# Sums, differences and residuals around the block products: from GpSimd to VectorE

## The chip, the cores and the metric

One core of one Trainium2 chip runs the whole program. A core has TensorE (PE, matrix products), VectorE (DVE), ScalarE (ACT), GpSimd (POOL), SyncE (SP, which here issues the DMAs), an on-chip memory SBUF, and the banks PSUM into which TensorE writes. Each engine takes its instructions in one fixed order and waits at each until its inputs are there. The metric is device time in microseconds (us) of one execution, less is better.

## The reference

One layer of a hybrid decoder for 2048 tokens of width 1024, in float32:

```python
h = rms_norm(x, norm_mix) * (1 + sc1) + sh1        # shifts, scales, gates from silu(c) @ w_ada
z = h @ w_in                                       # 1024 -> q, k, v of 12 + 4 heads, and two gates
ya = dilated_mixture(qa, ka, va) @ w_up_a          # windowed attention, three dilations, merged
yb = forgetting_attention(qb, kb, vb, fz, b_forget) @ w_up_b
x = x + g1 * ((sigmoid(gza) * ya + sigmoid(gzb) * yb) @ w_out)
h = rms_norm(x, norm_ffn) * (1 + sc2) + sh2
gate, up = split(h @ w_ffn_in)                     # 1024 -> 2 x 2816
x = x + g2 * ((silu(gate) * up) @ w_ffn_out)       # 2816 -> 1024
out = rms_norm(x, norm_final)
```

## The kernel before

Five phases follow each other: 1, the projection by `w_in`; 2, the two attentions and their merge; 3, `w_out` with the residual and the second norm; 4, `w_ffn_in` with silu; 5, `w_ffn_out` with the residual and the last norm.

**Precision.** A float32 operand is split into a high part, rounded by ScalarE (line 108), and a low part, the rest, which VectorE subtracts (line 109, `split`). A product then takes three matmuls (lines 102 to 104, `mm3`).

**Seven products for eight.** Phases 1, 3, 4 and 5 multiply 2x2 blocks with seven block products in place of eight (Strassen's scheme in Winograd's form). The price is sums and differences of blocks before and after the products.
- On the resident side, `a_prep` makes seven operands A11, A12, S1, S2, S3, A22, S4 of (usually) four 128x512 tiles each. Such a *preparation* is 28 splits, and per tile the sum for S1 (line 181), two differences on the way to S2 and S3 (183, 185) and two for S4 (192). There is one at each of: the start of phase 1 (tiles `a_`, written out at lines 353 to 376), its second half, phase 3 (`wo_`), the two halves of phase 4 (`f_`), and the three thirds of phase 5 (`w_`; the first with three tiles for four). The code gives a slot to every resident tile once, so a preparation writes a tile as soon as the products of the stage before have read it.
- On the streamed side, `b_ops` makes for each block four differences `wt` (line 219) and splits seven operands into `wh` and `wl`. Of `wh` and of `wl` there are six slots, so splits run at most six products ahead. One product is 12 matmuls of 512 columns, one block 84.
- Behind the products, ScalarE copies partial sums out of PSUM (`keep`, line 246: `p`, `u`), VectorE adds them to later ones. In phases 3 and 5 `residual` adds the old `x` to the copy (line 1026) and then to the product (1027); in phase 4 `up_` multiplies by the silu (1098).
- `scaled` loads a tile `ws` of an output weight, multiplies it by a gate (line 566) and stores it, eight rows in the gate blocks of phase 1, 22 in phase 4.

**Who does what.** In the kernel before GpSimd makes S1's sum and S3's difference, all `wt`, the `scaled` products, the residual's first sum, the silu's product, and the low part of one tile in each preparation of phase 4. In phase 2 it makes attention biases (815, 820) and parts of the merge (966, 968, 992).

**Order.** The program is traced in the order of the code and then put in order by a scheduler that works with its own estimates of times. The same code with an operation on another engine is thus put in another order, on all engines.

Of the kernel before, what the change touches and what calls it, by code (L numbers as in the profile page):

```python
# [37 lines left out]

PRODUCTS = {1: "A11", 2: "A12", 3: "S4", 4: "A22", 5: "S1", 6: "S2", 7: "S3"}
ORDER = (1, 2, 5, 6, 7, 4, 3)  # L40

GL4 = (("A11", 3),)

SEGS = {"A": ("pc",), "F": ("wh", "wl")}
SCT = {"A": "X", "F": "Z", "E": "XZ", "U": "X"}
# [16 lines left out]
def trunk(ctx, tc, x, c, w_ada, b_ada, norm_mix, w_in, b_forget, w_up_a, w_up_b, w_out,  # L62
# [40 lines left out]
        PE.matmul(o, lh, rl, start=False, stop=False, skip_group_check=True)  # L103
        PE.matmul(o, ll, rh, start=False, stop=last, skip_group_check=True)  # L104

    def split(hi, lo, src, sub=None):

        A.activation(hi, src, AF.Copy)  # L108
        (sub or V).tensor_tensor(lo, src, raw(hi), op=ALU.subtract)  # L109

    def rstd_of(ss, n, nm):

# [54 lines left out]
            t.setdefault(n, []).append(slot("big" if i < 11 else "bigx", nm + n + s, [P, nk, CH], F32R))  # L167
        return t

    def a_prep(t, get, nk=4, gl=()):  # L170


        def sp(n, k, p):
            split(t[n][0][:, k, :], t[n][1][:, k, :], p, G if (n, k) in gl else None)
        for k in range(nk):
            sp("A11", k, get(0, k))
        for k in range(nk):
            sp("A12", k, get(0, k + nk))
        for k in range(nk):
            pb, pb4, pa, s1 = get(1, k), get(1, k + nk), get(0, k), slot("pc", "s1")  # L180
            G.tensor_tensor(s1, pb, pb4, op=ALU.add)
            sp("S1", k, s1)
            V.tensor_tensor(s1, s1, pa, op=ALU.subtract)  # L183
            sp("S2", k, s1)
            G.tensor_tensor(pb, pa, pb, op=ALU.subtract)
            sp("S3", k, pb)
        for k in range(nk):
            sp("A22", k, get(1, k + nk))
        for k in range(nk):
            p = get(0, k + nk)  # L190
            for part in t["S2"]:
                V.tensor_tensor(p, p, raw(part)[:, k, :], op=ALU.subtract)  # L192
            sp("S4", k, p)
# [15 lines left out]
    def b_ops(groups, shape, lockstep=False):  # L209

        f = lambda a: a[:, :shape[0] * shape[1]].rearrange("p (a b) -> p a b", a=shape[0])
        vs = [{1: b11, 2: b21, 3: b22} for b11, b21, b12, b22 in groups]
        made = {5: lambda g, v: (g[2], g[0]), 6: lambda g, v: (g[3], v[5]), 7: lambda g, v: (g[3], g[2]),
                4: lambda g, v: (g[1], v[6])}

        def make(i, g, v):
            if i in made:
                v[i] = f(slot("wt", f"wt{i}"))
                G.tensor_tensor(v[i], *made[i](g, v), op=ALU.subtract)  # L219
        if len(groups) == 1 or not lockstep:  # L220
            for g, v in zip(groups, vs):
                for i in (5, 6, 7, 4):
                    make(i, g, v)
        ops = [{} for _ in groups]
        for i in ORDER:
            for g, v, o in zip(groups, vs, ops):
                if i not in v:
                    make(i, g, v)
                o[i] = f(slot("wh", "wh", dt=F32R)), f(slot("wl", "wl", dt=F32R))
                split(*o[i], v[i])  # L230
        return ops
# [129 lines left out]
    for k in range(4):  # L361
        for kk in (k, k + 4):
            A.activation(pb[kk], x_t(xb, kk), AF.Identity, bias=S1[:, kk:kk + 1], scale=A1[:, kk:kk + 1])
        G.tensor_tensor(s1[k], pb[k], pb[k + 4], op=ALU.add)
        sp("S1", k, s1[k])
    for k in range(4):
        V.tensor_tensor(s1[k], s1[k], pa[k], op=ALU.subtract)
        sp("S2", k, s1[k])
    for k in range(4):
        G.tensor_tensor(pb[k], pa[k], pb[k], op=ALU.subtract)  # L370
        sp("S3", k, pb[k])
    for k in range(4):
        sp("A22", k, pb[k + 4])
# [185 lines left out]
    def scaled(w, dst, k, row, hold_):  # L559

        for n in range(2):
            ns = slice(n * CH, (n + 1) * CH)
            p = slot("pc", "ws")
            with tc.issue_after(hold_):
                SP.dma_start(p, w[k * P:(k + 1) * P, ns])
            G.tensor_tensor(p, p, row[n], op=ALU.mult)  # L566
            SP.dma_start(dst[k * P:(k + 1) * P, ns], p)

    for i, (jL, jR) in enumerate(QK_PAIRS):
# [450 lines left out]
    def residual(xs, o, kept, i, n, out_=None):  # L1020

        xt = xs[i][n]
        if kept is None:
            V.tensor_tensor(xt, o, xt, op=ALU.add)
        else:
            G.tensor_tensor(kept, kept, xt, op=ALU.add)  # L1026
            V.tensor_tensor(xt, o, kept, op=ALU.add)  # L1027
        return xt

# [46 lines left out]
    for hf in range(2):  # L1076
        at4 = a_tiles(f"f{hf}_")
        a, b = 2 * hf, 2 * hf + 1
        a_prep(at4, from_dram(h2sp, a, b), gl=GL4)

        def p4_block(f):
            sil = {}

            def c11(o, kept):
                t = slot("s", "ga")
                V.tensor_tensor(t, o, kept, op=ALU.add)
                A.activation(t, t, AF.Silu)
                sil["a"] = t

            def c21(o):  # L1090
                t = slot("s", "gb")
                A.activation(t, o, AF.Silu)  # L1092
                sil["b"] = t

            def up_(o, kept, ci, which):
                t = slot("t", "ac")
                V.tensor_tensor(t, o, kept, op=ALU.add)  # L1097
                G.tensor_tensor(t, t, sil[which], op=ALU.mult)  # L1098
                SP.dma_start(act_scr[ci][f], t)
            return (kcols(w_ffn_in, f * P, P), kcols(w_ffn_in, DFF + f * P, P),  # L1100
                    c11, lambda o, t: up_(o, t, a, "a"), c21, lambda o, t: up_(o, t, b, "b"))
# [90 lines left out]
```

## Time and profile before

| | |
|---|---|
| median of three runs | 2989.59 us (2987.12 to 2991.21) |
| profiled execution, its own time | 2990.01 us |
| its span (first to last instruction) | 2988.30 us |
| TensorE busy | 2789.4 us, 93% |
| VectorE busy | 1906.6 us, 64% |
| ScalarE busy | 1371.7 us, 46% |
| GpSimd busy | 1359.1 us, 45% |

Busy time of an engine is the union of its instructions' spans. TensorE is without work for 199 us of the span; the mean hides that these lie in a few stretches.

### The profile page before, as it was taken

What the parts mean: (1) busy time and instruction counts of PE and PEld (TensorE: products, weight loads), DVE (VectorE), ACT (ScalarE), POOL (GpSimd) and SP (SyncE); (2) the same over time, 40 slices, a digit from 0 to 9 for tenths busy, and PEclk for the clock granted to TensorE, in tenths of its full rate; (3) what the DMA queues carried; (4) which work ended last, traced back from release to release, by engine and by line L of the source; (5) the groups of instructions that cost most, each with busy time, mean ns of one, the idle gap of its engine ahead of it and who ended that gap; (6) DMA issues with size and microseconds to landing.
All of it is one profiled execution on the core that took longest, in us unless ns stands there. A gap on an engine that the chain in (4) does not pass through costs nothing.

```text
span 2988.3 us, 41178 instructions
## 1 busy us (share of the span) xinstructions
PE 2789.4 (93%) x13666; PEld 2311.8 (77%) x13666; DVE 1906.6 (64%) x3509; ACT 1371.7 (46%) x2722; POOL 1359.1 (45%) x1077
## 2 busy tenths in 40 slices
PE   4899999999999999788798999999999999989898
PEld 3689887978887889676586788887788887868676
DVE  7865478476537887787667744337633338694987
ACT  3554335344447777652355533334333334433443
POOL 2323234323532222654645565545644436564642
PEclk7999999999999999999899999999999999989999
DMA  7487466467856757479566544444422236775642
GB/s 247 121 219 224 131 208 195 145 169 190 266 183 241 238 182 241 115 223 327 192 206 205 182 152 138 141 141 138 138 85 85 85 102 196 216 229 162 194 155 96
DMA packets 488414, 530.54 MB, mean 178 GB/s; under 512 B 58596, under 2 KB 339580, under 8 KB 481276
## 3 DMA queue, kind: packets, MB, share of 16 engines
q1 hardware_dynamic: 488200, 527.91, 56.4%
q8 instruction: 107, 1.75, 0.2%
q14 instruction: 107, 0.88, 0.1%
HBM read 356.51 MB, written 171.29 MB: 177 GB/s over the span
## 4 chain that ended last, share of the span: by engine, by line
PE 41%; DVE 6%; issue 2%; DMA 2%; POOL 1%; ACT 1%; SPq 0%; DVEq 0%; POOLq 0%; ACTq 0%
PE psX L102 8%; PE psX L103 8%; PE psX L104 7%; PE psZ L102 4%; PE psZ L104 4%; PE psZ L103 4%; PE psY L103 2%; PE psY L102 2%; PE psY L104 2%; DVE wl L109 1%; DVE pc L192 1%; POOL wt L219 1%; DMA x<-x 1%; DVE s L183 0%; DVE x L1027 0%
## 5 line engine op out<-in xcount | busy, mean ns | idle before, releaser
L109 DVE TENSOR_TENSOR wl<-wt,wh 128x512 fp32r<-128x512 f32 (+1 forms) x464 | 396.2, 859 | 414.8 <-ACT wh L108 388.8
L108 ACT ACTIVATE wh<-wt 128x512 fp32r<-128x512 f32 (+1 forms) x464 | 288.1, 622 | 622.1 <-PE psX L103 273.7
L219 POOL TENSOR_TENSOR wt<-wr,wt 128x512 f32<-128x512 f32 (+1 forms) x216 | 319.5, 1480 | 402.8 <-DVE wl L109 339.5
L219 POOL TENSOR_TENSOR wt<-wr 128x512 f32<-128x512 f32 (+1 forms) x216 | 310.7, 1438 | 286.8 <-DVE wl L109 222.3
L109 DVE TENSOR_TENSOR wl<-wr,wh 128x512 fp32r<-128x512 f32 (+1 forms) x324 | 274.7, 851 | 209.8 <-ACT wh L108 199.0
L108 ACT ACTIVATE wh<-wr 128x512 fp32r<-128x512 f32 (+1 forms) x324 | 201.1, 621 | 414.1 <-PE psX L103 233.5
L815 POOL TENSOR_SCALAR bi<-nf,F_col 128x512 f32<-128x512 f32 (+3 forms) x160 | 106.8, 671 | 232.4 <-DVE mx L829 204.9
L1026 POOL TENSOR_TENSOR u<-u,x 128x512 f32<-128x512 f32 x64 | 92.9, 1455 | 93.5 <-ACT u L246 83.8
L246 ACT ACTIVATE u<-psX 128x512 f32<-128x512 f32 x216 | 125.5, 581 | 5.8 <-PE psX L104 5.8
L1098 POOL TENSOR_TENSOR ac<-ac,gb 128x512 f32<-128x512 f32 x44 | 61.2, 1390 | 139.3 <-ACT gb L1092 139.3
L1097 DVE TENSOR_TENSOR ac<-psZ,u 128x512 f32<-128x512 f32 x88 | 60.4, 686 | 89.2 <-PE psZ L104 89.0
L839 ACT ACTIVATE L<-L,nmf 128x512 f32<-128x512 f32 (+3 forms) x160 | 103.3, 648 | 19.2 <-DVE nmf L835 19.2
L1098 POOL TENSOR_TENSOR ac<-ac,ga 128x512 f32<-128x512 f32 x44 | 73.6, 1672 | 52.3 <-DVE ac L1097 52.3
L871 PE MATMUL psY<-ph,vhl 128*128 128x256 f32 (+1 forms) x288 | 82.0, 299 | 5.2 <-ACT ph L108 4.1
L871 PE MATMUL psY<-pl,vhl 128*128 128x256 f32 (+1 forms) x288 | 80.9, 310 | 3.1 <-DVE pl L109 2.6
L737 DVE CUSTOM_DVE_ANT_0 L<-psX,bias 128x128 f32<-128x128 f32 (+1 forms) x192 | 64.7, 357 | 23.6 <-PE psX L736 21.7
L1027 DVE TENSOR_TENSOR x<-psZ,u 128x512 f32<-128x512 f32 x64 | 43.8, 685 | 56.0 <-PE psZ L104 28.3
L566 POOL TENSOR_TENSOR ws<-ws,g2b 128x512 f32<-128x512 f32 x44 | 66.5, 1534 | 28.0 <-DMA ws<-in_w_ffn_out_dram 21.6
L773 PE MATMUL psY<-pf,va 128*65 128x128 f32 (+1 forms) x408 | 77.8, 324 | 0.6 <-DVE pf L769 0.2
L745 ACT ACTIVATE L<-L,nm 128x128 f32<-128x128 f32 (+1 forms) x192 | 72.3, 450 | 9.5 <-DVE nm L740 9.3
L102 PE MATMUL psZ<-y,wu 128*128 128x512 f32 x128 | 55.5, 434 | 22.3 <-DVE gt L991 16.6
L108 ACT ACTIVATE ph<-psT 128x512 fp32r<-128x512 f32 (+1 forms) x101 | 56.6, 569 | 41.5 <-PE psT L863 40.8
(532 smaller groups left out, 9236.3 us busy)
## 6 DMA issues: line engine op xcount, KB each, us to landing
x<-x SPq DMA_DIRECT2D x192, 256.0 KB
wr<-in_w_ffn_in_dram SPq DMA_DIRECT2D x88, 512.0 KB
wr<-in_w_in_dram SPq DMA_DIRECT2D x64, 512.0 KB
qk<-sh SPq DMA_DIRECT2D x192, 128.0 KB
act<-ac SPq DMA_DIRECT2D x88, 256.0 KB
pc<-wfg SPq DMA_DIRECT2D x77, 256.0 KB
qk<-st SPq DMA_DIRECT2D x128, 128.0 KB
wa<-in_w_ada_dram SPq DMA_DIRECT2D x64, 256.0 KB
```

The costliest lines, as they stand in the source:

```text
L102: PE.matmul(o, lh, rh, start=first, stop=False, skip_group_check=True)
L103: PE.matmul(o, lh, rl, start=False, stop=False, skip_group_check=True)
L104: PE.matmul(o, ll, rh, start=False, stop=last, skip_group_check=True)
L108: A.activation(hi, src, AF.Copy)
L109: (sub or V).tensor_tensor(lo, src, raw(hi), op=ALU.subtract)
L219: G.tensor_tensor(v[i], *made[i](g, v), op=ALU.subtract)
L246: A.activation(t, o, AF.Copy, scale=1.0 if scale is None else scale)
L815: G.tensor_scalar(bi[:, :e - sg], nf[sg // D][:, sg % D:sg % D + e - sg], 1.0, F_col[:, qb * NHB + h:qb * NHB + h + 1], op0=ALU.mult, op1= ...
L839: A.activation(Ls[cq, b, sg][:, :e - sg], Ls[cq, b, sg][:, :e - sg], AF.Exp, bias=nm, accum_out=dp[:, i:i + 1])
L871: PE.matmul(uo[:, q0:256], vhl[:, kb, :], p_[:, 256 * i:256 * i + 256 - q0], start=(kp == 0 and i == 0 and j == 0), stop=(last and i == 1 ...
L1026: G.tensor_tensor(kept, kept, xt, op=ALU.add)
L1098: G.tensor_tensor(t, t, sil[which], op=ALU.mult)
```

## The change

Every one of the operations named above moves from GpSimd to VectorE, except those of phase 2. Nothing is computed otherwise. 772 instructions move: GpSimd has 1082 before and 310 after, VectorE 3511 and 4283 (branches counted).

```diff
-GL4 = (("A11", 3),)
...
-    def split(hi, lo, src, sub=None):
+    def split(hi, lo, src):
         A.activation(hi, src, AF.Copy)
-        (sub or V).tensor_tensor(lo, src, raw(hi), op=ALU.subtract)
+        V.tensor_tensor(lo, src, raw(hi), op=ALU.subtract)
...
-            split(t[n][0][:, k, :], t[n][1][:, k, :], p, G if (n, k) in gl else None)
+            split(t[n][0][:, k, :], t[n][1][:, k, :], p)
...
             pb, pb4, pa, s1 = get(1, k), get(1, k + nk), get(0, k), slot("pc", "s1")
-            G.tensor_tensor(s1, pb, pb4, op=ALU.add)
+            V.tensor_tensor(s1, pb, pb4, op=ALU.add)
             sp("S1", k, s1)
             V.tensor_tensor(s1, s1, pa, op=ALU.subtract)
             sp("S2", k, s1)
-            G.tensor_tensor(pb, pa, pb, op=ALU.subtract)
+            V.tensor_tensor(pb, pa, pb, op=ALU.subtract)
             sp("S3", k, pb)
...
                 v[i] = f(slot("wt", f"wt{i}"))
-                G.tensor_tensor(v[i], *made[i](g, v), op=ALU.subtract)
+                V.tensor_tensor(v[i], *made[i](g, v), op=ALU.subtract)
...
-            G.tensor_tensor(p, p, row[n], op=ALU.mult)
+            V.tensor_tensor(p, p, row[n], op=ALU.mult)
             SP.dma_start(dst[k * P:(k + 1) * P, ns], p)
...
-            G.tensor_tensor(kept, kept, xt, op=ALU.add)
+            V.tensor_tensor(kept, kept, xt, op=ALU.add)
             V.tensor_tensor(xt, o, kept, op=ALU.add)
...
                 V.tensor_tensor(t, o, kept, op=ALU.add)
-                G.tensor_tensor(t, t, sil[which], op=ALU.mult)
+                V.tensor_tensor(t, t, sil[which], op=ALU.mult)
```

(The two sums of the first preparation, lines 364 and 370, change in the same way.) Lines after the change carry numbers lower by two: 109 is 107, 219 is 217, 566 is 564.

How the order moves is shown at two places. The first is VectorE in the preparation of the second half of phase 4: `f1_A12l` are low parts of the resident tiles, `wl` those of streamed operands, and `ga` reads a product out of PSUM and lets ScalarE go on. Before:

```order
L109 TENSOR_TENSOR wl_20829<-wt7_20826,wh_20828 128x512
L109 TENSOR_TENSOR wl_20835<-wt7_20832,wh_20834 128x512
L109 TENSOR_TENSOR wl_20841<-wt4_20838,wh_20840 128x512
L109 TENSOR_TENSOR f1_A12l_21073<-pc_21100,f1_A12h_21072 128x512
L109 TENSOR_TENSOR f1_A12l_21073<-pc_21104,f1_A12h_21072 128x512
L109 TENSOR_TENSOR f1_A12l_21073<-pc_21108,f1_A12h_21072 128x512
L1086 TENSOR_TENSOR ga_20919<-psY_20876,p1_20890 128x512
L109 TENSOR_TENSOR f1_A12l_21073<-pc_21112,f1_A12h_21072 128x512
```

and after, up to the same `ga`:

```order
L1096 TENSOR_TENSOR ac_20766<-ac_20766,ga_20693 128x512
L183 TENSOR_TENSOR pc_21116<-pc_21120,pc_21116 128x512
L107 TENSOR_TENSOR wl_20835<-wt7_20832,wh_20834 128x512
L217 TENSOR_TENSOR wt5_21250<-wr_21226,wr_21224 128x512
L217 TENSOR_TENSOR wt6_21256<-wr_21222,wt5_21244 128x512
L107 TENSOR_TENSOR wl_20841<-wt4_20838,wh_20840 128x512
L107 TENSOR_TENSOR f1_A12l_21073<-pc_21100,f1_A12h_21072 128x512
L217 TENSOR_TENSOR wt6_21262<-wr_21226,wt5_21250 128x512
L107 TENSOR_TENSOR f1_A12l_21073<-pc_21104,f1_A12h_21072 128x512
L107 TENSOR_TENSOR f1_A12l_21073<-pc_21108,f1_A12h_21072 128x512
L1084 TENSOR_TENSOR ga_20919<-psY_20876,p1_20890 128x512
L107 TENSOR_TENSOR f1_A12l_21073<-pc_21112,f1_A12h_21072 128x512
```

The old instructions keep their order, and the moved ones (1096, 183, 217) stand between them.

The second place is the end of the projection of queries and keys in phase 1, where `scaled` begins. `ws_7567` and `ws_7719` are tiles of the output weight, `st` with `psZ` reads a product out of PSUM. VectorE after:

```order
L107 TENSOR_TENSOR wl_7045<-wr_7010,wh_7044 128x512
L415 SCALAR_TENSOR_TENSOR st_6974<-psZ_6873,u3_6949 128x512
L107 TENSOR_TENSOR wl_7190<-wr_7177,wh_7189 128x512
L564 TENSOR_TENSOR ws_7567<-ws_7567,g1b_7412 128x512
L107 TENSOR_TENSOR st_6963<-st_6963,sh_6965 128x512
L107 TENSOR_TENSOR st_6974<-st_6974,sh_6976 128x512
L624 TENSOR_SCALAR fx_7354<-psT_7392 64x128
L107 TENSOR_TENSOR wl_7194<-wr_7177,wh_7193 128x512
L564 TENSOR_TENSOR ws_7719<-ws_7719,g1b_7411 128x512
L415 SCALAR_TENSOR_TENSOR st_6997<-psZ_6873,u2_6935 128x512
```

Before, the two `ws` were not in this queue. SyncE, which issues their loads, before, behind the stores of `qk14`:

```order
L422 DMA qk14_125<-sh_7248 64x512
L628 DMA nf_230<-fx_7354 4x128 x2
L567 DMA wog_233<-ws_7563 128x512
L565 DMA ws_7567<-in_w_out_dram 128x512
L240 DMA wr_7571<-in_w_in_dram 128x8x128
L240 DMA wr_7573<-in_w_in_dram 128x8x128
L565 DMA ws_7719<-in_w_out_dram 128x512
```

and after, behind those of `qk10`:

```order
L420 DMA qk10_121<-st_6900 64x512
L420 DMA qk10_121<-sh_6902 64x512
L565 DMA wog_233<-ws_7563 128x512
L563 DMA ws_7567<-in_w_out_dram 128x512
L238 DMA wr_7571<-in_w_in_dram 128x8x128
L238 DMA wr_7573<-in_w_in_dram 128x8x128
L563 DMA ws_7719<-in_w_out_dram 128x512
L420 DMA qk10_121<-sh_6965 64x512 x3
```

The loads stand 38 rows of SyncE's order earlier.

## Rows read from the trace of the kernel before

**Rows 1.** Windows: length, busy us and count of PE, PEld, DVE, ACT, POOL; PEclk, DMA.

```profile
40.00:112.00 72.00, 43.04 (x145) 29.92 (x146) 65.19 (x102) 35.56 (x68) 36.95 (x21) 0.74 0.33 91
1440.00:1492.00 52.00, 37.22 (x129) 27.14 (x128) 39.45 (x49) 20.15 (x39) 34.43 (x18) 0.80 0.41 128
1597.00:1682.00 85.00, 71.62 (x306) 56.89 (x305) 78.13 (x125) 51.27 (x103) 42.70 (x27) 0.90 0.63 200
2049.00:2118.00 69.00, 59.93 (x245) 47.67 (x244) 68.10 (x66) 33.05 (x61) 43.98 (x27) 0.95 0.51 162
2481.00:2532.00 51.00, 48.03 (x207) 38.21 (x206) 48.94 (x53) 26.90 (x53) 33.34 (x24) 1.00 0.70 224
2610.00:2682.00 72.00, 56.97 (x222) 44.77 (x221) 69.11 (x69) 29.32 (x54) 52.70 (x33) 0.88 0.75 238
2775.00:2876.00 101.00, 89.38 (x373) 72.15 (x372) 95.12 (x143) 44.47 (x88) 61.66 (x39) 0.95 0.59 181
1700.00:2049.00 349.00, 349.00 (x1542) 289.05 (x1541) 145.30 (x186) 127.98 (x224) 206.41 (x147) 1.00 0.44 143
```

**Rows 2.** Timeline of ScalarE, VectorE, TensorE at 2050: start, length, instruction, count, [idle before].

```profile
2050.61 5.17 DVE L109 TENSOR_TENSOR f_A12l<-pc,f_A12h 128x512 fp32r<-128x512 f32 x3
2056.41 0.63 ACT L1087 ACTIVATE ga<-ga 128x512 f32<-128x512 f32 x1 [3.84 <-DVE ga L1086]
...
2058.10 0.50 PE L102 MATMUL psX<-f_S3h,wh 128*128 128x512 f32 x1 [1.93 <-ACT u L246]
```

**Rows 3.** Timeline of VectorE, GpSimd and TensorE at 1465 to 1486.

```profile
1464.99 1.28 DVE L109 TENSOR_TENSOR wo_A22l<-pc,wo_A22h 128x512 fp32r<-128x512 f32 x2
...
1469.43 8.84 POOL L219 TENSOR_TENSOR wt<-wr,wt 128x512 f32<-128x512 f32 x1 [9.39 <-DVE wl L109]
1478.23 1.28 POOL L1026 TENSOR_TENSOR u<-u,x 128x512 f32<-128x512 f32 x1
...
1484.42 0.69 DVE L1027 TENSOR_TENSOR x<-psZ,u 128x512 f32<-128x512 f32 x1 [7.30 <-POOL u L1026]
...
1485.16 0.79 PE L102 MATMUL psZ<-wo_S4h,wh 128*128 128x512 f32 x1 [5.64 <-DVE x L1027]
```

**Rows 4.** Groups of the whole span: busy us, mean ns, idle before.

```profile
L1097 DVE TENSOR_TENSOR ac<-psZ,u 128x512 f32<-128x512 f32 x88 | 60.4, 686 | 89.2 <-PE psZ L104 89.0
```

**Rows 5.** Windows, line 109 alone: length, busy us and count of DVE, of POOL.

```profile
40.00:112.00 72.00, 33.05 (x44) 0.00 (x0) 0.74 0.33 91
1440.00:1492.00 52.00, 28.36 (x31) 0.00 (x0) 0.80 0.41 128
1597.00:1682.00 85.00, 41.37 (x49) 1.80 (x1) 0.90 0.63 200
2049.00:2118.00 69.00, 53.31 (x45) 0.00 (x0) 0.95 0.51 162
2481.00:2532.00 51.00, 38.12 (x37) 0.00 (x0) 1.00 0.70 224
2610.00:2682.00 72.00, 50.37 (x44) 0.00 (x0) 0.88 0.75 238
2775.00:2876.00 101.00, 59.42 (x55) 0.00 (x0) 0.95 0.59 181
```

**Rows 6.** The same windows, sums for line 183 (21 instructions) and for 192 (46).

```profile
sum 502.00, DVE 22.86; mean DVE 3.27
...
sum 502.00, DVE 40.16; mean DVE 5.74
```

**Rows 7.** Timeline of VectorE at 42.

```profile
42.50 6.24 DVE L356 TENSOR_SCALAR xt<-xt,A,S 128x512 f32<-128x512 f32 x5
```

**Rows 8.** Timeline of SyncE, VectorE and GpSimd at 721 to 760.

```profile
721.54 1.85 SPq L628 DMA_DIRECT2D nf<-fx  x5
...
723.12 0.68 DVE L109 TENSOR_TENSOR wl<-wr,wh 128x512 fp32r<-128x512 f32 x1
...
759.00 1.29 POOL L566 TENSOR_TENSOR ws<-ws,g1b 128x512 f32<-128x512 f32 x1 [22.91 <-DMA ws<-in_w_out_dram]
```

More of the change, by code (lines that the diff above doesn't have):

```diff
@@ L168, in a_tiles, with a_prep @@
         return t
-    def a_prep(t, get, nk=4, gl=()):
+    def a_prep(t, get, nk=4):
         def sp(n, k, p):
-            split(t[n][0][:, k, :], t[n][1][:, k, :], p, G if (n, k) in gl else None)
+            split(t[n][0][:, k, :], t[n][1][:, k, :], p)
         for k in range(nk):
@@ L363, in trunk @@
             A.activation(pb[kk], x_t(xb, kk), AF.Identity, bias=S1[:, kk:kk + 1], scale=A1[:, kk:kk + 1])
-        G.tensor_tensor(s1[k], pb[k], pb[k + 4], op=ALU.add)
+        V.tensor_tensor(s1[k], pb[k], pb[k + 4], op=ALU.add)
         sp("S1", k, s1[k])
@@ L369, in trunk @@
     for k in range(4):
-        G.tensor_tensor(pb[k], pa[k], pb[k], op=ALU.subtract)
+        V.tensor_tensor(pb[k], pa[k], pb[k], op=ALU.subtract)
         sp("S3", k, pb[k])
@@ L1078, in trunk @@
         a, b = 2 * hf, 2 * hf + 1
-        a_prep(at4, from_dram(h2sp, a, b), gl=GL4)
+        a_prep(at4, from_dram(h2sp, a, b))
         def p4_block(f):
```

## The prediction

> **What bounds the kernel now.** I first cut the span into windows. In a steady stretch of phase 4 TensorE works 349.00 of 349 us while VectorE is busy for 145.30 and GpSimd for 206.41 [rows 1]: there nothing that happens on those two engines costs time. One of its matmuls takes 349.00 / 1542 = 0.226 us. The loss sits in the seven preparations, whose windows come first in the same view: 502 us, TensorE busy for 406.19 (the sum of its column), so 95.8 us idle, about half of what it idles in the whole span. In the same windows VectorE is busy for 464.0 us, 92%, so it has 38 us to spare. Where TensorE idles there, VectorE or something behind it is late.
>
> The timeline shows how. At 2050.61 three low parts of A12 take VectorE 5.17 us; behind them in its queue stands the addition `ga`, ScalarE waits 3.84 us for that, and TensorE 1.93 us for the copy `u` that ScalarE makes next [rows 2]. That is 1.72 us for one subtraction. Its own price is in another stretch: two in a row take 1.28 us [rows 3] and one alone 0.68 [rows 8], so the second adds 0.60. Additions of the same size that read one input from PSUM show a mean of 686 ns over the whole span [rows 4]. So the instruction is not slow: a VectorE operation with both inputs in SBUF is lengthened, here by 1.72 - 0.60 = 1.1 us, and what is active beside it in these stretches is GpSimd (305.8 of the 502 us, the sum of its column).
>
> It also goes the other way. At 1469.43 a GpSimd difference `wt` takes 8.84 us where a GpSimd sum takes 1.28; the residual sum in its queue thereby comes late, VectorE's addition `x` waits 7.30 us for it, and TensorE 5.64 for that [rows 3].
>
> **The change part by part.** All sums go against the profiled execution, 2990.01 us (span 2988.30 and 1.71 around it); the median of the runs is 0.4 us lower, so no correction is made.
>
> *Relief of the subtractions.* Line 109 on VectorE takes 304.0 us for 305 instructions in the seven windows [rows 5]. At 0.60 each that would be 183.0: 121.0 less.
>
> *Relief of the differences that stay.* Lines 183 and 192 have 21 and 46 instructions with 22.86 and 40.16 us [rows 6]: 63.0 - 67 x 0.60 = 22.8 less.
>
> *What is added.* GpSimd has 189 instructions in these windows [rows 1]; three belong to the merge and stay, so 189 is a little high. Their price on VectorE is not in the trace, since VectorE makes no such sum before, but 183 and 192 are the same operation on the same tiles: between 0.60 (behind another) and 0.68 (alone) [rows 3, 8]. In a queue that is 92% busy most stand behind another, so I take 0.60: 113.4 more. Net for VectorE in the windows: 121.0 + 22.8 - 113.4 = 30.4 us less. At 0.68 throughout, for the old and the new, it would be 304.0 + 63.0 - 561 x 0.68 = -14 us, a loss of 14, which the 38 us of spare time can take. Those are the two bounds of the sum. Put another way, one GpSimd instruction costs VectorE 143.8 / 189 = 0.76 us of waiting beside it, and 0.60 if VectorE makes it itself. The gain is thin per instruction.
>
> The Trainium skill (Perfetto Trace Analysis, Optimizing Scalar/DVE Operations) gives about 60 ns of data-access overhead of a VectorE instruction on SBUF as engine-busy time, with profiled latency about twice that, since the second half overlaps the next instruction. By that I estimate the pitch at 0.68 - 0.06 = 0.62 us, and the net relief at 304.0 + 63.0 - 561 x 0.62 = 19 us for 30. The two rows say 0.60, and the sum goes by them.
>
> *Further relief.* Five scale-and-shift operations of line 356 take 6.24 us at 42.5 [rows 7]; at the 0.60 of an equal tile (an estimate) it would be 3.2 less. They stand ahead of all splits of the first preparation, so all of it is on the path. The GpSimd queue behind the 8.84 us `wt` no longer exists: TensorE's 5.64 us at 1479 go.
>
> *Sum.* 30.4 + 3.2 + 5.6 = 39.2, with VectorE's time in the windows counted in full on the path, since it is what is waited for. 2990.0 - 39.2 is about **2950 us**.
>
> *What is costed at nothing.* Outside the preparations the moved instructions fill VectorE's spare time: in the steady stretch 147 x 0.60 = 88 us on top of 145.3, of 349. The slots for `wh` and `wl` let splits run six products ahead, 6 x 12 x 0.226 = 16 us, so a delay of a few us there does not reach TensorE. The silu's product and its store follow the products and nobody waits for them soon. `scaled` outside the place below, likewise. The low part that GpSimd made in phase 4's preparations is among the 189. TensorE's granted clock is 0.74 to 1.00 of its upper level of 2.4 GHz in the windows and 1.00 in the steady stretch [rows 1], and a TensorE that waits less may get it back; since VectorE sets the end there, I count nothing.
>
> *A wait that is added.* `scaled` waits for a load, and VectorE now waits in order. Before, the low part `wl` ahead of its place ran at 723.12, while GpSimd got its first `ws` only at 759.00, after 22.91 us of idleness for that DMA [rows 8]. Behind `ws` on VectorE are now the residues of `st`, `fx`, and the `wl` on which TensorE depends. But the loads too stand 38 rows of SyncE's order earlier, about where `nf` was issued at 721.54 [rows 8], and so should have landed some 2 to 4 us behind the `wl`. The 16 us of split-ahead cover that: nothing.
>
> **The rivals.**
>
> A, *the load comes late after all.* If SyncE is held up at that place, by a store that waits or by the tile's slot in `pc`, and the load lands as before at about 759, VectorE stands for 35 us. TensorE has 16 us of operands, so it loses 19: 2950 + 19 = 2969. For it: the order is strict, and the 22.91 us are in the trace. Against: the rows ahead of the load are only stores of tiles already made by then.
>
> B, *VectorE becomes the bound, slower.* Place: the preparations. If the lengthening isn't GpSimd's doing but that of something that stays (the DMAs or ScalarE's traffic beside it), nothing is relieved, and 113.4 us of added work meet 38 us of spare time: 75 us more, 2990 + 75 = 3065. It decides once the relief per subtraction falls below (113.4 - 38) / 305 = 0.25 us instead of the 121.0 / 305 = 0.40 that I count. For it: VectorE is 92% busy there and the price of the cure is nearly that of the illness. Against: 1.7 us do not appear in additions from PSUM, which wait with the same DMAs around [rows 4].
>
> Beside B stands the Trainium skill, Perfetto Trace Analysis, Optimizing Scalar/DVE Operations: where VectorE is saturated, handing work to another engine, even GpSimd, may make sense, which speaks against this change. The same place adds that moving work between these two might not help, since they share a port; the 5.17 and the 8.84 us [rows 2, 3] are of that second kind.
>
> C, *nothing much.* The stalls in the preparations belong to ScalarE's 28 high parts, the loads and the order in which slots come free; VectorE's relief then shows as idle time of VectorE, and only the 5.6 us of the held residual return: 2984. For it: ScalarE's wait in [rows 2] is one of many, and a preparation is also limited by the products that free its tiles. Against: VectorE at 92%, ScalarE at 35.56 of 72 in the first window and 33.05 of 69 at 2049 [rows 1].
>
> **How the numbers follow.** Forecast 71%, A 9%, B 12%, C 8%. The predicted time is the forecast's. Downwards the range takes in that VectorE's 38 us of idleness go too, since part of it is spent waiting for GpSimd: 2950 - 38 = 2912. (If TensorE idled nowhere in the windows it would be 2990 - 96 = 2894, which I leave out, as the first operands of a preparation can't come before its tiles.) Upwards it takes in A, and C with the 4 us between the runs of before: 2988. The dear price of 0.68, taken up by the spare time, lies with C. B is left out. 0.2% is 6 us, about what a measurement of this kernel can tell from no change: forecast and A are faster (0.80), C straddles that bound and with the edges of the others gives 0.08, B 0.12 slower.
>
> **What the changed profile would show.** Right: line 107 (109 before) in the preparations with a mean near 0.65 where it was 1.0; GpSimd nearly idle outside phase 2; TensorE's idle time in the seven preparations near 96 - 39 = 57 us; VectorE's busy time in them near 434, though it makes 186 instructions more; the steady stretches still full. The three A12 parts at the start of the second half of phase 4 take about 1.9 us for 5.17. VectorE shows no wait of over some 4 us for a `ws` near 724. Wrong: a VectorE idle of tens of us for the DMA of `ws` with TensorE idle behind it (A); subtractions still over 1 us with GpSimd silent (B); subtractions at 0.65 and TensorE's idle time the same, now ended by ScalarE or DMA (C). Most of all the forecast falls if the order that the scheduler makes from its own times puts moved sums ahead of splits for which TensorE waits: then VectorE is faster, and still late at the one place that counts.

## The result, and the profile after

The changed kernel takes 2907.81 us (median of four runs, 2903.23 to 2908.12) against 2988.76 before: a ratio of 0.972, interval 0.9708 to 0.9732. That is 81 us less, twice the 39 that were forecast, and 4 us below the lower end of the range (2912). The profiled execution has a span of 2905.8 us, 82.5 less than before; TensorE is busy for 2771.8 us of it, VectorE for 2047.5, GpSimd for 217.4.

The windows over the same seven preparations, cut at the same matmuls as in [rows 1] (counted off in TensorE's order), now read:

```profile
41.00:100.30 59.30, 42.52 (x146) 30.09 (x147) 56.55 (x123) 34.53 (x67) 0.00 (x0) 0.74 0.41 118
1424.20:1465.60 41.40, 33.77 (x129) 25.00 (x129) 39.27 (x64) 20.15 (x41) 5.62 (x2) 0.88 0.51 163
1572.30:1645.80 73.50, 69.25 (x306) 55.09 (x305) 68.06 (x148) 49.30 (x98) 0.00 (x0) 0.98 0.68 222
2013.20:2068.30 55.10, 55.10 (x244) 45.61 (x243) 55.05 (x92) 33.57 (x61) 0.00 (x0) 1.00 0.60 192
2431.40:2477.90 46.50, 46.50 (x207) 38.48 (x206) 43.52 (x78) 27.00 (x53) 0.00 (x0) 1.00 0.76 242
2554.70:2616.00 61.30, 54.13 (x221) 42.51 (x220) 59.18 (x99) 29.37 (x53) 0.00 (x0) 0.94 0.81 261
2709.00:2794.50 85.50, 84.40 (x373) 69.55 (x372) 79.42 (x173) 44.20 (x88) 0.00 (x0) 1.00 0.60 186
sum 422.60, PE 385.67 PEld 306.33 DVE 401.06 ACT 238.13 POOL 5.62; mean PE 55.10 PEld 43.76 DVE 57.29 ACT 34.02 POOL 0.80
```

Nearly all of the gain is here: 502.0 - 422.6 = 79.4 us. Seen from TensorE it is 58.9 us of idle time (95.8 to 36.9) and 20.5 of busy time: the same matmuls (1627 and 1626) take 385.7 for 406.2 us, because the granted clock, in the column PEclk, rises in five of the seven windows, for example from 0.80 to 0.88 in the second and from 0.95 to 1.00 in the fourth. Seen from VectorE the same 79.4 us are 63.0 of busy time (464.0 to 401.1), though it makes 170 instructions more, and 16.4 of idle time (38.0 to 21.5). Of these 16.4, 10.4 lie in the second window, where VectorE's busy time hardly changed (39.45 and 39.27).

A steady stretch of phase 4 in the same view, with VectorE busier than in [rows 1] (61% for 42%) and TensorE as full:

```profile
1700.00:2013.00 313.00, 313.00 (x1382) 259.18 (x1381) 190.64 (x295) 115.34 (x201) 0.00 (x0) 1.00 0.42 138
```

The timeline of ScalarE and VectorE at the place of [rows 2], the second half of phase 4:

```profile
2014.03 0.69 DVE L107 TENSOR_TENSOR f_A12l<-pc,f_A12h 128x512 fp32r<-128x512 f32 x1
...
2015.23 1.29 DVE L107 TENSOR_TENSOR f_A12l<-pc,f_A12h 128x512 fp32r<-128x512 f32 x2
...
2016.44 0.68 DVE L1084 TENSOR_TENSOR ga<-psY,p 128x512 f32<-128x512 f32 x1
...
2017.16 0.64 ACT L1085 ACTIVATE ga<-ga 128x512 f32<-128x512 f32 x1 [0.24 <-DVE ga L1084]
```

The three low parts that took 5.17 us take 1.98, and ScalarE waits 0.24 us for `ga` where it waited 3.84, although moved instructions now stand between them in VectorE's queue.

Two groups of rows show what the forecast left out. First the small steps of the norm and the scaling of rows in the third window (1597 to 1682), groups of VectorE by line, before; the last columns are count, busy us, mean ns of one, idle before:

```profile
L1060 DVE TENSOR_SCALAR x<-x,rs_r 128x512 f32<-128x512 f32 x12 | 10.3, 918 | 0.1
L121 DVE TENSOR_TENSOR rs_t<-rs_t,rs_v 128x2 f32<-128x2 f32 x9 | 2.5, 282 | 0.2
L120 DVE SCALAR_TENSOR_TENSOR rs_t<-rs_r 128x2 f32<-128x2 f32 x9 | 2.5, 281 | 0.2
L122 DVE SCALAR_TENSOR_TENSOR rs_r<-rs_t,rs_r 128x2 f32<-128x2 f32 x9 | 2.5, 280 | 0.2
```

and after, in the same stretch (1572.3 to 1645.8):

```profile
L1058 DVE TENSOR_SCALAR x<-x,rs_r 128x512 f32<-128x512 f32 x8 | 3.3, 483 | 0.0
L118 DVE SCALAR_TENSOR_TENSOR rs_t<-rs_r 128x2 f32<-128x2 f32 x9 | 1.4, 160 | 0.0
L119 DVE TENSOR_TENSOR rs_t<-rs_t,rs_v 128x2 f32<-128x2 f32 x9 | 1.4, 160 | 0.0
L120 DVE SCALAR_TENSOR_TENSOR rs_r<-rs_t,rs_r 128x2 f32<-128x2 f32 x8 | 1.2, 160 | 0.0
```

An instruction on 128x2 numbers was 0.12 us longer on average while GpSimd worked beside it, and a scaling of 128x512 took 0.92 us for 0.48.

A mean hides how the time was lost. Of the 372 subtractions of lines 109, 183 and 192 in the seven windows of before, 228 took about 0.7 us, their own price, and 94 took 1.7 to 1.8; 44 lie between and six were smaller ones. So most were left alone, and a quarter were lengthened by 1.0 to 1.1 us each.

### The profile page after: what moved, and what is told of

Same layout as the page of the kernel before. It is cut to its first block, busy times and chain, and to the rows that moved or that the text cites. A ratio compares the mean times of both kernels' runs of the same rounds, so it can differ in the third digit from the quotient of the medians.

```text
span 2905.8 us, 40608 instructions
## 1 busy us (share of the span) xinstructions
PE 2771.8 (95%) x13666; PEld 2303.4 (79%) x13666; DVE 2047.5 (70%) x4281; ACT 1378.9 (47%) x2722; POOL 217.4 (7%) x305
## 4 chain that ended last, share of the span: by engine, by line
PE 45%; DVE 3%; DMA 1%; issue 1%; ACT 1%; POOLq 0%; DVEq 0%; SPq 0%; ACTq 0%
PE psX L100 9%; PE psX L101 9%; PE psX L102 8%; PE psZ L100 4%; PE psZ L101 4%; PE psZ L102 4%; PE psY L101 2%; PE psY L100 2%; PE psY L102 2%; DMA x<-x 1%; DVE wl L107 1%; DVE wt L217 0%; PE psT L1065 0%; DMA out_dram<-x 0%; DVE x L1025 0%
## 5 line engine op out<-in xcount | busy, mean ns | idle before, releaser
L107 DVE TENSOR_TENSOR wl<-wt,wh 128x512 fp32r<-128x512 f32 (+1 forms) x464 | 314.4, 681 | 260.6 <-ACT wh L106 240.7
L107 DVE TENSOR_TENSOR wl<-wr,wh 128x512 fp32r<-128x512 f32 (+1 forms) x324 | 220.2, 680 | 192.6 <-ACT wh L106 171.1
L217 DVE TENSOR_TENSOR wt<-wr 128x512 f32<-128x512 f32 (+1 forms) x216 | 147.8, 684 | 12.5 <-DMA wr<-in_w_in_dram 6.6
L217 DVE TENSOR_TENSOR wt<-wr,wt 128x512 f32<-128x512 f32 (+1 forms) x216 | 147.0, 681 | 3.7
L837 ACT ACTIVATE L<-L,nmf 128x512 f32<-128x512 f32 (+3 forms) x160 | 103.6, 650 | 19.7 <-DVE nmf L833 19.4
L869 PE MATMUL psY<-pl,vhl 128*128 128x256 f32 (+1 forms) x288 | 82.5, 314 | 2.4 <-DVE pl L107 1.6
L107 DVE TENSOR_TENSOR pl<-psT,ph 128x512 fp32r<-128x512 f32 (+1 forms) x101 | 64.9, 646 | 20.0 <-ACT ph L106 19.6
L100 PE MATMUL psX<-f_A11h,wh 128*128 128x512 f32 x176 | 69.3, 394 | 0.0
L102 PE MATMUL psX<-f_A11h,wl 128*128 128x512 f32 x176 | 68.9, 392 | 0.0
L100 PE MATMUL psZ<-f_S4h,wh 128*128 128x512 f32 x176 | 68.7, 390 | 0.2 <-DVE ac L1095 0.2
L101 PE MATMUL psX<-f_A11l,wh 128*128 128x512 f32 x176 | 68.9, 392 | 0.0
```

The costliest lines, as they stand in the source:

```text
L100: PE.matmul(o, lh, rh, start=first, stop=False, skip_group_check=True)
L107: V.tensor_tensor(lo, src, raw(hi), op=ALU.subtract)
L217: V.tensor_tensor(v[i], *made[i](g, v), op=ALU.subtract)
L837: A.activation(Ls[cq, b, sg][:, :e - sg], Ls[cq, b, sg][:, :e - sg], AF.Exp, bias=nm, accum_out=dp[:, i:i + 1])
L869: PE.matmul(uo[:, q0:256], vhl[:, kb, :], p_[:, 256 * i:256 * i + 256 - q0], start=(kp == 0 and i == 0 and j == 0), stop=(last and i == 1 ...
```

## The experiments

Three theories were set against each other. Theory 1, *lengthening*: GpSimd at work beside VectorE makes VectorE's own instructions longer, and VectorE bounds the preparations. Theory 2, *lateness*: GpSimd's results came late, and the gain is that of waits for them. Theory 3, *order*: the change put all engines' instructions in another order, and that is what counts.

| kernel | median us | to before, with interval |
|---|---|---|
| changed kernel | 2907.81 | 0.9720 (0.9708 to 0.9732) |
| sums_only | 2966.01 | 0.9918 (0.9903 to 0.9933) |
| wt_only | 2941.15 | 0.9834 (0.9819 to 0.9849) |
| rest_only | 2965.94 | 0.9914 (0.9898 to 0.9931) |
| spare_one | 2915.50 | 0.9751 (0.9736 to 0.9765) |
| spare_two | 2937.28 | 0.9822 (0.9808 to 0.9837) |
| spare_four | 3012.26 | 1.0079 (1.0064 to 1.0094) |
| late_fill | 2911.65 | 0.9738 (0.9721 to 0.9754) |
| gts_V | 2904.45 | 0.9718 (0.9701 to 0.9736) |
| merge_V | 2922.63 | 0.9774 (0.9759 to 0.9789) |
| act_scale | 2896.54 | 0.9689 (0.9675 to 0.9704) |

The runs of before beside them had medians of 2988.8 to 2990.4 us.

### One part of the change alone

sums_only, against the changed kernel:

```diff
-                V.tensor_tensor(v[i], *made[i](g, v), op=ALU.subtract)
+                G.tensor_tensor(v[i], *made[i](g, v), op=ALU.subtract)
-            V.tensor_tensor(p, p, row[n], op=ALU.mult)
+            G.tensor_tensor(p, p, row[n], op=ALU.mult)
-            V.tensor_tensor(kept, kept, xt, op=ALU.add)
+            G.tensor_tensor(kept, kept, xt, op=ALU.add)
-                V.tensor_tensor(t, t, sil[which], op=ALU.mult)
+                G.tensor_tensor(t, t, sil[which], op=ALU.mult)
```

> Only the sums of the preparations (S1, S3, the two of the first preparation, the low part of phase 4) are on VectorE; wt, scaled, the residual's first sum and the silu's product stay on GpSimd. Theory 1, lengthening: GpSimd in use beside VectorE lengthens every VectorE instruction that works in SBUF, by about 0.9 us for each GpSimd instruction, and all of the gain of 81 us comes in proportion to the instructions taken away in the seven preparations: 47 of 186, so 20 us, about 2969. Theory 2, lateness: TensorE and VectorE waited for GpSimd's results in the chain S1, S2, S3, so that moving just these brings more than half, 2945 or less. Theory 3, order: what counts is the new order of the instructions; no number follows, but parts need not add up to 81 us.

wt_only, against the kernel before:

```diff
-                G.tensor_tensor(v[i], *made[i](g, v), op=ALU.subtract)
+                V.tensor_tensor(v[i], *made[i](g, v), op=ALU.subtract)
```

> Only the differences wt of the streamed side are on VectorE. Theory 1, lengthening: 89 of the 186 GpSimd instructions of the preparations go, 38 us, about 2951. Theory 2, lateness: if the chain is that of the preparation's sums, next to nothing, 2980 to 2990; if it is the wt that come late, most of the 81 us, 2925 or less. Theory 3, order: no number follows.

rest_only, against the kernel before:

```diff
-            G.tensor_tensor(p, p, row[n], op=ALU.mult)
+            V.tensor_tensor(p, p, row[n], op=ALU.mult)
-            G.tensor_tensor(kept, kept, xt, op=ALU.add)
+            V.tensor_tensor(kept, kept, xt, op=ALU.add)
-                G.tensor_tensor(t, t, sil[which], op=ALU.mult)
+                V.tensor_tensor(t, t, sil[which], op=ALU.mult)
```

> Only scaled, the residual's first sum and the silu's product are on VectorE. Theory 1, lengthening: 48 of the 186 GpSimd instructions of the preparations go, 21 us, about 2968. Theory 2, lateness: TensorE's waits for x behind a late residual go (5.6 and 6.3 us in the trace of before), 2977 or so. Theory 3, order: no number follows.

The three gain 24.3, 49.1 and 24.3 us, where shares by the number of instructions gave 20, 38 and 21. No part carries nearly the whole, and none next to nothing, as theory 2 had it, and the order of the three sizes is that of the counts. Together they make 97.7 us for the 81 of the whole change: each alone gains somewhat more than its share, so the gains are not quite additive. That alone doesn't refute theory 3.

### Contention put back, with no change of order and almost nothing to wait for

spare_two, against the changed kernel:

```diff
+    spare = cst.tile([P, 384], F32, name="spare")
...
                 V.tensor_tensor(v[i], *made[i](g, v), op=ALU.subtract)
+                n = min(shape[0], 384 // shape[1])
+                o = spare[:, :n * shape[1]].rearrange("p (a b) -> p a b", a=n)
+                G.tensor_tensor(o, v[i][:, :n], v[i][:, :n], op=ALU.add)
```

> The changed kernel, with one more GpSimd instruction behind each wt: it adds the wt to itself (two SBUF inputs, 384 columns) into a tile that nobody reads. The rows of TensorE, ScalarE and VectorE are in the same order as in the changed kernel, and no result of GpSimd is waited for in the preparations. Theory 1, lengthening: about 84 of these stand in the preparations and cost VectorE 0.75 x 0.9 us each, 57 us, of which its idle time there (22 us) may take some: 2945 to 2965, with subtractions of VectorE above 0.8 us there. Theory 2, lateness, and theory 3, order: no change from the changed kernel, 2905 to 2912.

spare_four does the addition twice:

```diff
-                G.tensor_tensor(o, v[i][:, :n], v[i][:, :n], op=ALU.add)
+                for _ in range(2):
+                    G.tensor_tensor(o, v[i][:, :n], v[i][:, :n], op=ALU.add)
```

> As spare_two, with the idle addition done twice behind each wt: some 170 of them in the preparations, nearly as many as GpSimd had instructions there before (186), and again the same order on TensorE, ScalarE and VectorE as in the changed kernel. Theory 1: twice the 29.5 us of spare_two or a little more, 2960 to 2975, with VectorE's subtractions near 0.7 us and its small instructions of the norms above 0.25. Theories 2 and 3: as the wait for a free wt slot, if that was behind the 29.5 us, grows with a queue: no bound, but VectorE's busy time stays near 433.

spare_two loses 29.5 us of the 81 and spare_four all of it: 3012.26 us, slower than before. The sums over the seven preparations, of spare_two:

```profile
sum 446.80, PE 393.65 PEld 308.04 DVE 433.00 ACT 238.15 POOL 147.03; mean PE 56.24 PEld 44.01 DVE 61.86 ACT 34.02 POOL 21.00
```

and of spare_four:

```profile
sum 492.00, PE 406.15 PEld 315.48 DVE 477.80 ACT 239.34 POOL 232.49; mean PE 58.02 PEld 45.07 DVE 68.26 ACT 34.19 POOL 33.21
```

VectorE's busy time rises from 401.1 to 433.0 and 477.8 us though it makes no instruction more (765 and 762 in these windows for 777), and the preparations go from 422.6 to 446.8 and 492.0. TensorE's busy time goes back to 406.2 too, by its clock (granted 0.90 in the third window of spare_four, for 0.98). In the traces of the changed kernel, spare_two and spare_four, TensorE, ScalarE and VectorE make the same instructions in the same order, from the first to the last. VectorE's waits for GpSimd, for the slot of a `wt` that the idle addition still reads, come to 3.7 us in spare_four's whole span and do not appear in spare_two. In spare_four's timeline of VectorE, at the A12 parts once more, the lengthening is there instruction by instruction:

```profile
2063.17 0.68 DVE L218 TENSOR_TENSOR wt<-wr,wt 128x512 f32<-128x512 f32 x1
2063.77 1.31 DVE L107 TENSOR_TENSOR wl<-wt,wh 128x512 fp32r<-128x512 f32 x1
2065.01 1.31 DVE L107 TENSOR_TENSOR f_A12l<-pc,f_A12h 128x512 fp32r<-128x512 f32 x1
```

So lengthening is shown to be enough for a loss of this size, with the order of the changed kernel on TensorE, ScalarE and VectorE; theory 3 is not needed for it. The price was missed, though: 29.5 us where 37 to 57 were expected, and then 104.5 for 52 to 67. One idle addition of three quarters of the size costs VectorE (433.0 - 401.1) / 87 = 0.37 us in the one and 76.7 / 168 = 0.46 in the other. Part of spare_two's falls into VectorE's idle time there, which drops from 21.5 to 13.8 us and stays at 14.2 in spare_four. Of the 104.5 us some 35 lie outside the preparations, 22 of them in four stretches (from 100, 512, 2068 and 2478 us of the changed kernel on) where that kernel kept TensorE full. There spare_two cost 1.7 us in all, and spare_four brought TensorE 3.1 to 4.6 us of idle time in each. So one price for each GpSimd instruction doesn't carry over from few of them to many.

### The same with one input

spare_one, in place of spare_two's addition:

```diff
-                G.tensor_tensor(o, v[i][:, :n], v[i][:, :n], op=ALU.add)
+                G.tensor_scalar(o, v[i][:, :n], 1.0, 0.0, op0=ALU.mult, op1=ALU.add)
```

> As spare_two, but the idle GpSimd instruction behind each wt reads it once (scale and shift, one SBUF input, 384 columns). Theory 1: as spare_two took 29.5 us more than the changed kernel, this takes as much if what counts is that GpSimd is at work in SBUF, 2930 to 2940, and nothing if only its two inputs count, 2905 to 2912. Theory 2, lateness: as spare_two shows lengthened subtractions already, no number.

7.7 us more than the changed kernel, a quarter of spare_two's: neither of the two that were expected. So most of spare_two's loss comes with the second input of the GpSimd instruction; whether through the input itself or through the longer time that the instruction takes was not separated.

### Bare instructions

The kernel micro leaves out the layer. It runs one VectorE instruction many times, first alone and then beside 20 GpSimd instructions on other tiles.

> Nothing of the layer is computed: rows of one VectorE instruction run alone, and then beside 20 equal GpSimd instructions on tiles that have nothing to do with them. Theory 1, lengthening: beside GpSimd additions of two SBUF inputs (1.28 us each) a VectorE subtraction of two SBUF inputs goes from a pitch of 0.60 to 1.2 or more, and so do the scale-and-shift with two columns and the small products of 128x4 (0.1 us alone, above 0.2 beside it), which the forecast left out; VectorE additions with one input from PSUM stay at 0.60 to 0.69. Whether GpSimd with one SBUF input, or with a fill that reads nothing, does the same isn't known: between 0.60 and 1.7. Theory 2 and 3: no VectorE instruction becomes longer by itself.

Its timeline, first VectorE's subtraction of two SBUF inputs (line 39), alone, beside GpSimd's additions (line 54), beside its scale and shift with one input (57), and beside its fill (60); the last row has GpSimd's additions practically alone:

```profile
5.81 17.41 DVE L39 TENSOR_TENSOR vo<-va,vb 128x512 f32<-128x512 f32 x24
...
23.45 24.75 DVE L39 TENSOR_TENSOR vo<-va,vb 128x512 f32<-128x512 f32 x16
...
24.28 31.74 POOL L54 TENSOR_TENSOR go<-ga,gb 128x512 f32<-128x512 f32 x20
...
62.14 15.62 DVE L39 TENSOR_TENSOR vo<-va,vb 128x512 f32<-128x512 f32 x16
...
62.98 18.76 POOL L57 TENSOR_SCALAR go<-ga 128x512 f32<-128x512 f32 x20
...
87.84 11.59 DVE L39 TENSOR_TENSOR vo<-va,vb 128x512 f32<-128x512 f32 x16
...
88.65 11.58 POOL L60 MEMSET go<- 128x512 f32 x20
...
106.34 10.84 DVE L42 TENSOR_TENSOR vo<-pa,vb 128x512 f32<-128x512 f32 x15
...
106.73 26.74 POOL L54 TENSOR_TENSOR go<-ga,gb 128x512 f32<-128x512 f32 x20
...
140.30 13.96 DVE L48 TENSOR_SCALAR vo<-va,ta,tb 128x512 f32<-128x512 f32 x24
...
154.50 27.45 DVE L48 TENSOR_SCALAR vo<-va,ta,tb 128x512 f32<-128x512 f32 x20
...
185.69 9.39 DVE L51 TENSOR_TENSOR to<-ta,tb 128x4 f32<-128x4 f32 x48
...
195.32 28.39 DVE L51 TENSOR_TENSOR to<-ta,tb 128x4 f32<-128x4 f32 x48
...
195.71 26.81 POOL L54 TENSOR_TENSOR go<-ga,gb 128x512 f32<-128x512 f32 x20
...
225.04 26.72 POOL L54 TENSOR_TENSOR go<-ga,gb 128x512 f32<-128x512 f32 x20
```

Divided by the counts: the subtraction takes 0.73 us alone, 1.55 beside the additions, 0.98 beside the scale and shift, 0.72 beside the fill. With one input from PSUM (line 42) it stays at 0.72 beside the additions, and these take 1.34 us each, as alone, where beside two SBUF inputs they take 1.59. The scale and shift with two columns goes from 0.58 to 1.37, and the product of 128x4 numbers, the kind that the forecast left out, from 0.20 to 0.59: three times its price. (Alone the subtraction is at 0.73 and not at 0.60, perhaps since all write one tile; that was not tried.)

The Trainium skill (SBUF — State Buffer, Who interferes with whom) says that a VectorE instruction with two SBUF inputs contends with a GpSimd instruction that reads SBUF and not with one that only writes, that one SBUF input outside certain modes doesn't contend, and that scalings can enter those modes; these runs agree in each of these. The same page (Summary: rules for kernel authors) says that the second of such a pair to issue blocks fully until the first finishes. By that I estimate a pair at 0.73 + 1.34 = 2.07 us; measured, a pair takes 1.55 to 1.59, so about half a microsecond of the two still runs side by side.

The kernel before has a place where the loss falls wholly on GpSimd. While the difference `wt` of [rows 3] took its 8.84 us, from 1469.43 to 1478.27, VectorE ran 12 instructions without a gap, each at its own price. Two of them, the later one the last:

```profile
1470.41 0.68 DVE L192 TENSOR_TENSOR pc<-pc,wo_S2l 128x512 f32<-128x512 f32 x1
...
1476.43 0.68 DVE L109 TENSOR_TENSOR wl<-wr,wh 128x512 fp32r<-128x512 f32 x1
```

The difference ended 1.2 us after that one had. So which of the two engines pays is not fixed, and no run here shows what decides it.

### Lateness alone

late_fill, against the changed kernel, with the same fill of `pb` behind S3's difference. The fills replace a quarter of the values of these sums, so it doesn't compute the layer:

```diff
                 V.tensor_tensor(v[i], *made[i](g, v), op=ALU.subtract)
+                for _ in range(4):
+                    G.memset(v[i][:, shape[0] - 1, :P], 0.5)
...
             V.tensor_tensor(s1, pb, pb4, op=ALU.add)
+            for _ in range(4):
+                G.memset(s1[:, :P], 0.5)
```

> The changed kernel, but behind each wt and behind each sum for S1 and S3 of the preparations (not the first one's) GpSimd fills the last or first 128 columns of the result with 0.5, four times over, and whoever reads the result waits for that. So these sums come late by a GpSimd queue again, while a fill did not lengthen VectorE's subtractions in the kernel of bare instructions (0.72 us each with and without it). A quarter of the values of these sums is thereby replaced. The seven preparations lost 79.6 us by the change, 62.8 in VectorE's busy time and 16.8 in its idle time. Theory 1, lengthening makes the first and lateness at most the second: 2908 to 2925, VectorE's busy time in the preparations near 400 us. Theory 2, lateness makes most: above 2945.

2911.65 us, 3.8 more than the changed kernel in the medians, with intervals that overlap (0.9721 to 0.9754, and 0.9708 to 0.9732), and in the range of theory 1. The sum over its preparations:

```profile
sum 432.80, PE 387.19 PEld 306.09 DVE 400.19 ACT 236.41 POOL 101.02; mean PE 55.31 PEld 43.73 DVE 57.17 ACT 33.77 POOL 14.43
```

VectorE's busy time is that of the changed kernel and its idle time 11 us longer; ScalarE's high parts of the streamed side wait 229 us in total for the filled `wt`, and TensorE idles 45.6 us in the preparations for 36.9. Four fills take 4 x 0.2 = 0.8 us, half of what a GpSimd sum took before, and the order of the rows is not quite that of the changed kernel, so this is no measure of the whole lateness of before. A bound for that comes from VectorE's account: lateness shows there as idle time, so theory 2 makes at most 16.4 of the 79.4 us. In the waits of before, 10.9 us of VectorE's idle time in the seven windows end with a GpSimd result (7.3, 2.4 and 1.2 us, all at line 1027); in the changed kernel's windows it is 1.2, for a sum of the merge.

### The same idea carried further

gts_V moves the merge's additions (line 990), merge_V its products and sums of 128x1024 as well:

```diff
-UM = ("GVGG", "GVGV")
-UA = ("GG", "VV")
+UM = ("VVVV", "VVVV")
+UA = ("VV", "VV")
...
-                G.tensor_tensor(gts[0], gts[0], gts[1], op=ALU.add)
+                V.tensor_tensor(gts[0], gts[0], gts[1], op=ALU.add)
```

(gts_V has the last of these two edits alone.)

> The changed kernel, and the 32 additions of the two gated halves (line 990) on VectorE too. In the merge (1182 to 1424 of the changed kernel's profile) VectorE is busy for 186.6 of 242 us and TensorE idles for 40.5, for gt 14.5 and for mx 13.2 of it. Theory 1, lengthening, as in the preparations: each costs VectorE 0.60 and gives back 0.7 to 0.9 us of lengthening, 3 to 10 us less, 2898 to 2905. Rival: here biases of GpSimd or the loads set the pace, 2905 to 2912.

> As gts_V, and the 14 products and sums of 128x1024 of the merge on VectorE as well, so that GpSimd is left with the biases alone. Theory 1: 14 times 2.4 us on GpSimd become 14 times some 1.2 on VectorE, and its other instructions there (wu 0.92, y 0.86, uw 1.62 us) go back to their own price: 5 to 20 us less than the changed kernel, 2888 to 2903. Rival: VectorE becomes the bound of the merge, 2908 to 2925.

gts_V is 3.4 us below the changed kernel in the medians, inside theory 1's range, but its ratio, 0.9718, is the same within the intervals. merge_V is 14.8 us slower than the changed kernel, against theory 1 and in the range of its rival, that VectorE becomes the bound of the merge. The windows of the merge, of the changed kernel and of merge_V, and merge_V's longest wait of VectorE in it (total us, times, longest):

```profile
1181.90:1424.20 242.30, 201.84 (x1015) 161.63 (x1015) 186.57 (x396) 110.78 (x256) 124.41 (x119) 0.92 0.74 231
...
1181.30:1436.90 255.60, 205.64 (x1015) 164.61 (x1015) 206.81 (x441) 111.70 (x257) 44.56 (x75) 0.90 0.71 218
...
DVE uw L964 <- DMA uw<-wrow: 16.2, 9, 4.2
```

VectorE's other instructions there did return to their own price (`wu` 0.68 for 0.92 us). Still its busy time in the merge grows by 20.2 us, its idle time falls by only 6.9, and the merge takes 255.6 us for 242.3. Its wait for these loads grows too, from 7.3 to 16.2 us: a product that waits for its load now stands in VectorE's queue ahead of everything else, as in rival A. Which of the two made the merge longer, the added work or the waits in order, was not separated.

act_scale takes the opposite way and gives work of VectorE to ScalarE:

```diff
-                V.tensor_scalar(xt[h], xt[h], rs[:, i:i + 1], None, op0=ALU.mult)
+                A.activation(xt[h], xt[h], AF.Copy, scale=rs[:, i:i + 1])
...
-        V.tensor_scalar(pa[k], pa[k], A1[:, k:k + 1], S1[:, k:k + 1], op0=ALU.mult, op1=ALU.add)
+        A.activation(pa[k], pa[k], AF.Identity, bias=S1[:, k:k + 1], scale=A1[:, k:k + 1])
...
-                V.tensor_scalar(xh, xh, rs[:, i:i + 1], None, op0=ALU.mult)
+                A.activation(xh, xh, AF.Copy, scale=rs[:, i:i + 1])
```

> The changed kernel, with the scalings of the rows in the two norms (lines 296 and 1058) and the scale-and-shift of line 354 on ScalarE. If VectorE's busy time bounds the preparations (401 of 422 us in the changed kernel, ScalarE 238), its 28 instructions there with some 11 us go, and the time falls by 5 to 11 us, 2897 to 2903. Rival: ScalarE's high parts stand in the same chain and get later by as much, 2905 to 2912.

2896.54 us, the fastest of all: 11.3 less than the changed kernel, and just past the lower end of what was expected (2897). Its first preparation in the windows:

```profile
38.40:93.60 55.20, 38.19 (x145) 26.79 (x146) 48.61 (x103) 46.73 (x88) 0.00 (x0) 0.82 0.45 126
```

VectorE's busy time there falls by 7.9 us (56.55 to 48.61), the stretch by 4.1, and it begins 2.6 us earlier. The other preparations together are unchanged (363.9 for 363.3 us), though the third holds moved scalings too. What is left, about half of what the two profiled executions differ by, lies between the first preparation and the end of the merge, where the order moved as well; that part has no cause shown.

## Why the prediction was wrong

The sign, the place and the mechanism were right, the size was not: 39 us of gain for 81. The forecast applied the mechanism to the subtractions and to one other line, where it held for the steps of the norms and the scalings too. By its steps:

- **The place.** Right: 79.4 of the 81 us are in the seven preparations, and the steady stretches still have TensorE full.
- **Relief of the subtractions.** About right. The view of [rows 5] counts an instruction that stands between other lines in full (0.68 us and not 0.60), so sums by line don't add up to VectorE's busy time. Counted in the trace from each start to the next, they do. So counted, line 109 (107 after) goes from 295.5 us for 305 to 184.1 for 310, 111.4 less where 121.0 was forecast; lines 183 and 192 from 59.1 to 39.7, 19.4 less for 22.8. In the view itself line 109 reads 304.0 and then

```profile
sum 422.60, DVE 200.01; mean DVE 28.57
```

which is 0.65 us each.
- **What is added.** Right: the 177 moved instructions that now stand in the windows take 106.3 us, 0.60 each, where 113.4 was forecast for 189. The lines that the forecast priced thus give 111.4 + 19.4 - 106.3 = 24.5 us, for 30.4.
- **Further relief: the step that failed.** The forecast gave 3.2 us to line 356 and nothing, without a reason, to the other VectorE instructions that are no subtractions. Counted in the same way, the steps of the norms (116 to 118, 120 to 122) go from 24.5 to 9.9 us, and the scalings and other sums (356, 367, 375, 1056, 1060, 1147, 1150) from 38.4 to 16.4: 36.6 us together, 3.9 of them at line 356, and some 3 of them because ten of the 151 instructions moved out of the windows. The bare instructions show that such instructions are lengthened, the smallest most of all for their size. This term is larger than the whole that the forecast took from VectorE's busy time.
- **The held residual.** Too small as well. The forecast took 5.6 us, a wait of TensorE's at one place, and had the rest of VectorE's idle time in its lower bound alone. VectorE's idle time fell by 16.4 us, 10.4 of it in the window of that place; 10.9 had ended with a GpSimd result. late_fill's preparations are 10 us longer than the changed kernel's, its whole time only 3.8.
- **Sum.** VectorE's busy time fell by 24.5 + 36.6 and 1.8 at other lines, 63.0 us in all (rounded). With 16.4 of idle time that is 79.4, where the forecast had 30.4 + 3.2 + 5.6.
- **TensorE's clock.** Counted at nothing. In two windows (2013.2 and 2431.4) TensorE is now full, at a clock of 1.00 (in the first of them VectorE too, with 55.05 of 55.10 us). At its clock of before, 0.95, its matmuls alone took the 59.93 us of [rows 1] in the first, more than the window's 55.1. So the clock did not add to the sum, but it let VectorE's relief through.
- **The wait at `ws`.** Right in the result: VectorE waits 2.10 and 2.01 us for the two tiles. But the forecast had misread its place: the GpSimd row at 759.00 belongs to the second `ws` of before, and the first had run at 709.99. The row of before, and two of after:

```profile
709.99 1.29 POOL L566 TENSOR_TENSOR ws<-ws,g1b 128x512 f32<-128x512 f32 x1 [9.08 <-DMA qk<-sh]
...
705.86 0.69 DVE L564 TENSOR_TENSOR ws<-ws,g1b 128x512 f32<-128x512 f32 x1 [2.10 <-DMA ws<-in_w_out_dram]
...
710.55 0.69 DVE L564 TENSOR_TENSOR ws<-ws,g1b 128x512 f32<-128x512 f32 x1 [2.01 <-DMA ws<-in_w_out_dram]
```

- **The rivals.** A did not come (waits of its kind are seen in merge_V). B fell with the mean of 0.65 us. C fell with TensorE's idle time, 36.9 us for 95.8.

What stays open: how much the new order itself is worth. With the order fixed, contention put back costs all that was gained; that order alone gives nothing was not shown. Of the idle part, how much is lateness and how much order is not shown either.

## What to carry to other kernels

Where one engine bounds a stretch, sum up everything on it that a neighbour lengthens, by the engine's total busy time in that stretch, and not only the lines that look alike: a tiny product of 128x4 was tripled by it. Work handed to a second engine that slows the first is not free: in the preparations one GpSimd instruction cost VectorE some (111.4 + 19.4 + 36.6) / 189 = 0.89 us of lengthening, and VectorE makes the same sum in 0.60. The move has an end: in the merge, where the moved products wait for loads and VectorE's queue stands behind them, more of it cost 14.8 us, by the added work or by these waits. Handing scalings to ScalarE instead gained 11.3 us, part of it at the place where VectorE was relieved.

## What was not expected

- The price of a GpSimd instruction to VectorE is not a constant: 0.37 us each with 87 idle additions in the preparations, 0.46 with 168. Nor does it fall evenly: a subtraction of before took 0.7 us or 1.7 to 1.8, and at one place GpSimd paid it all, with 8.84 us for one difference.
- A 128x4 product on VectorE goes from 0.20 to 0.59 us beside GpSimd additions, and GpSimd does not notice (26.81 us for 20, and 26.72 alone).
- TensorE's busy time moved with the idle time that VectorE left it, as its granted clock did: the same matmuls took 385.7, 393.7 and 406.2 us in the changed kernel, spare_two and spare_four.
